# Softmax attention on Trainium2: queries kept in an order by half and class modulo 4, and keys copied into that order on the chip

## The chip, the cores and the metric

The kernel runs on one NeuronCore of a Trainium2 chip. The metric is the device time of one execution in microseconds (us), here the median of three runs. The engines are TensorE (PE: matmuls; PEld: its weight loads), VectorE (DVE), ScalarE (ACT), GpSimd (POOL) and SyncE (SP, which issues most DMAs). Each engine works through its own instructions in program order.

## The reference, cut to what matters

One decoder layer: SwiGLU feed-forward, a mixing block, a second feed-forward, a gated per-layer embedding. The change touches the softmax attention over the prompt of 1024 tokens, with 8 heads of 64, which is half of the mixing block.

```python
DILATED_BRANCHES = ((128, 1), (512, 4), (2048, 16))
# a query at t reads t, t-d, t-2d, ..., t-window, in every branch; the branches are merged
# with weights proportional to their softmax denominators
for window, dil in DILATED_BRANCHES:
    o, l = dilated_branch_prompt(qa, ka, va, window, dil)
    outs.append(o)
    lses.append(l)
...
att = combine_branches(outs, lses)
```

So a query needs its near keys (distance up to 128, every one) and far keys at distances that are multiples of 4 (and of 16), that is, keys of its own class modulo 4. Merging by denominators lets the kernel add log-counts as a mask and use one softmax.

## The kernel before, in words

The program runs feed-forward 1 (to about 780 us), the projections and gated linear attention (to about 1127 us), the softmax attention of the prompt (about 1127 to 1300 us, eight heads one after the other), the output projection, feed-forward 2 and the embedding. Inside the mixing block PE, ACT, DVE and POOL follow an order written out by hand: generators ("streams") are merged by declared costs (`Merge`), and small pieces of work are put off by a number of steps with `L.add(steps, ...)` and run at the end of a step by `L.tick()`. SP is not in that hand-written order; a scheduler places its DMAs.

*Storing queries and keys.* Each projected chunk of 352 tokens arrives in PSUM. `store_qk` scales it into `t`, rotates it where needed, and ACT writes a rounded part `hi` (L935); one step later `spill_qk` subtracts on DVE to get `lo` (L942). After the third chunk of a group of 128 rows, `hi` and `lo` go to DRAM (`d_q`, `d_ql`, or `d_k`) by POOL DMAs (L947 to L951). There are four such groups each of keys and queries; the last group is of queries.

*Loading a head.* `load_a` brings `KA` (128 rows: the rounded part of the keys and their remainder) and `QA` (the rounded queries twice); `load_b` brings `KB` (rounded keys again; 8 more rows hold ones) and `QB` (remainder of the queries; 8 more rows hold the negative row maxima, written by POOL in `rows`, L1446). All of these are in the order of the tokens.

*Row maxima.* `max_step` makes 9 score tiles `sm` per head (L1420, queries as weights, keys moving); DVE reduces them; PE turns the result (`pm`, L1438), ACT copies it, POOL writes it into `QB`. This runs ahead of the main work by `LEAD` = 7 tiles beyond a whole head.

*Main work.* A head has 7 tiles (`TILES`), one per step. A tile is a PSUM bank `st` of keys by queries, filled by pairs of matmuls: `KA` by `QA` (L1472) and `KB` by `QB` (L1473), keys as weights and queries moving. Tiles 0, 1 and 4 are class tiles: parts `("c", half, r, w)` take the 128 keys of class r in one half of the sequence, and 256 or 128 queries of the class, both through `tokens_of`, which steps over 4 columns. Tiles 2, 3, 5 and 6 are near tiles: a block of 128 neighbouring keys and up to 256 neighbouring queries. One step later `weigh` adds the mask on DVE (L1483, L1485) and ACT takes the exponent (L1486). Two steps after the tile `total` multiplies with the values (L1499) into one of two PSUM banks `nd`, by 512 queries each; class parts write there with a step of 4 columns. `finish1` and `finish2` divide by the denominator: four ACT instructions (L1514 to L1521), two POOL products, one DVE and one ACT instruction, one POOL subtraction.

Beside it a stream `attend_sample` works on the cache of the 8 sample sequences; it streams `kc` and `vc` tiles of 448 KB by SP and multiplies them (L1608, L1656). The main work fills the rest of PE's order:

```python
        while done < min(len(maxes), NM + LEAD + (n + 1) * NM // len(TILES)):
            max_step(*maxes[done])
            done += 1
            t += 0.2
        L.tick()
```

## Time and profile before

| | |
|---|---|
| median of 3 runs | 2269.69 us (2266.19 to 2274.14) |
| the profiled execution's own time | 2270.06 us |
| its span, first to last instruction | 2268.3 us |
| mean granted TensorE clock | 0.982 |
| PE / PEld / DVE / ACT / POOL busy | 96% / 80% / 66% / 36% / 30% |
| DMA | 426 MB, mean 188 GB/s |

The busy shares are averages over stages with different limits. A PE that is busy all the time is not PE at its peak, since the ends of matmuls are modelled; the distance from one start to the next tells what an instruction costs. The profile shows the execution that was traced; its own time lies 0.4 us above the median.

### The profile page before, as it was taken

To read this page: it belongs to the slowest core of one execution; us is meant where nothing else is said; L and a number is where in the kernel's file an instruction comes from. 1 tells how busy PE (TensorE), PEld (TensorE's weight loads), DVE (VectorE), ACT (ScalarE), POOL (GpSimd) and SP (SyncE) were. 2 spreads that over 40 slices of the span, in tenths; PEclk is the share of its full clock that TensorE was granted. 3 is DMA by queue.
4 is the path that set the end of the run, shared out by engine and by line. 5 is a ranking of instruction groups with operands and counts; after the bars stand their busy time and mean duration, and the time that the engine had idled before them with its cause. 6 is when DMAs were issued, how large, how long until landed. Compare 5 with 4: busy or idle time off the path is not lost. (4 is left out here: it accounts for less than half of the span.)

```text
span 2268.3 us, 39818 instructions
## 1 busy us (share of the span) xinstructions
PE 2180.0 (96%) x16242; PEld 1812.5 (80%) x16242; DVE 1489.0 (66%) x2446; ACT 811.9 (36%) x1397; POOL 671.8 (30%) x490
## 2 busy tenths in 40 slices
PE   7999999999999999999999998999999999999896
PEld 5788888877777899889778896778888887777796
DVE  7855655568888835764367525865565658888947
ACT  4433333333112634433155503433333333111734
POOL 0456655550000001101044200265565551000225
PEclk9999999999999999989999998999999999999898
DMA  3376676659672211235978640277667639773212
GB/s 116 118 264 236 240 247 236 219 202 355 260 260 97 89 43 51 74 133 163 302 216 243 216 157 19 69 243 252 234 238 246 235 138 391 266 268 127 70 75 105
DMA packets 137832, 426.04 MB, mean 188 GB/s; under 512 B 17168, under 2 KB 38032, under 8 KB 126896
## 3 DMA queue, kind: packets, MB, share of 16 engines
q1 hardware_dynamic: 127616, 338.79, 42.6%
q0 software_dynamic: 4864, 80.09, 10.4%
q10 hardware_dynamic: 5168, 4.61, 0.6%
q8 instruction: 128, 2.10, 0.4%
q14 instruction: 56, 0.46, 0.1%
HBM read 313.73 MB, written 176.75 MB: 216 GB/s over the span
## 5 line engine op out<-in xcount | busy, mean ns | idle before, releaser
L174 PE MATMUL acc_a_f<-xxh_f,wh_f_a 128*128 128x512 f32 x704 | 225.0, 400 | 16.7 <-ACT xxh_f L239 11.3
L174 PEld LDWEIGHTS acc_a_f<-xxh_f,wh_f_a 128*128 128x128 f32 x704 | 133.5, 190 | 51.6 <-ACT xxh_f L239 13.0
L278 POOL TENSOR_TENSOR S_f<-raw_gu_f,S_f 128x512 f32<-128x512 f32 x40 | 59.4, 1485 | 324.2 <-DVE wl_f_a L293 324.2
L174 PE MATMUL acc_a_f<-xxh_f,wl_f_a 128*128 128x512 f32 x352 | 139.8, 397 | 0.0
L293 DVE TENSOR_TENSOR wl_f_a<-raw_gu_f,wh_f_a 128x1024 fp32r<-128x1024 f32 x44 | 56.0, 1275 | 117.1 <-ACT wh_f_a L292 117.1
L174 PE MATMUL acc_c_f<-xxl_f,wh_f_a 128*128 128x512 f32 x384 | 120.5, 395 | 0.0
L273 POOL TENSOR_TENSOR S_f<-raw_gu_f 128x512 f32<-128x512 f32 x40 | 54.4, 1359 | 222.6 <-DMA raw_gu_f<-w_gu 222.4
L351 ACT ACTIVATE g_f<-acc_a_f 128x512 f32<-128x512 f32 x44 | 26.3, 598 | 243.2 <-PE acc_a_f L174 241.8
L850 PE MATMUL acc_m<-wh_m,xh_mx 128*128 128x256 f32 x384 | 112.8, 294 | 0.0
L850 PE MATMUL acc_m<-wl_m,xh_mx 128*128 128x256 f32 x384 | 109.6, 285 | 0.0
L850 PE MATMUL acc_m<-wh_m,xl_mx 128*128 128x256 f32 x384 | 109.1, 284 | 0.0
L174 PE MATMUL acc_b_f<-xd_f,wh_f_s 128*128 128x512 f32 x320 | 102.5, 402 | 4.0 <-DVE c_f L335 4.0
L174 PE MATMUL acc_b_f<-xd_f,wh_f_a 128*128 128x512 f32 x320 | 104.2, 407 | 0.0
L174 PE MATMUL acc_b_f<-xc_f,wh_f_s 128*128 128x512 f32 x320 | 99.4, 392 | 2.1 <-DVE U_f L335 2.1
L174 PE MATMUL acc_c_f<-xxl_f,wh_f_s 128*128 128x512 f32 x320 | 100.2, 394 | 0.0
L546 ACT ACTIVATE wo_f_wl<-wr_f 128x1024 fp32r<-128x1024 f32 x36 | 38.1, 1059 | 155.9 <-DVE wr_f L335 62.5
L546 ACT ACTIVATE wo_f_wh<-wr_f 128x1024 fp32r<-128x1024 f32 x34 | 36.0, 1059 | 144.6 <-DVE wr_f L335 56.7
L174 PEld LDWEIGHTS acc_c_f<-xxl_f,wh_f_a 128*128 128x128 f32 x384 | 71.9, 188 | 17.0
L661 DVE SCALAR_TENSOR_TENSOR ho_f<-acc_d_f,ho_f 128x512 f32<-128x512 f32 x88 | 60.0, 689 | 33.8 <-PE acc_d_f L174 29.4
L354 ACT ACTIVATE g_f<-g_f 128x512 f32<-128x512 f32 x44 | 27.8, 633 | 148.9 <-DVE g_f L335 148.9
L293 DVE TENSOR_TENSOR wl_f_s<-S_f,wh_f_s 128x1024 fp32r<-128x1024 f32 x40 | 76.6, 1914 | 5.5 <-ACT wh_f_s L292 5.3
L174 PEld LDWEIGHTS acc_a_f<-xxh_f,wl_f_a 128*128 128x128 f32 x352 | 66.8, 190 | 15.9
(500 smaller groups left out, 6392.0 us busy)
## 6 DMA issues: line engine op xcount, KB each, us to landing
raw_gu_f<-w_gu SPq DMA_DIRECT2D x42, 1024.0 KB, 5.4
xo_f_xh<-d_hid SPq DMA_DIRECT2D x36, 1024.0 KB, 6.5
xo_f_xl<-d_hid SPq DMA_DIRECT2D x34, 1024.0 KB, 6.5
o_kw<-k_win POOLq DMA_DIRECT2D x8, 4088.0 KB, 15.8
o_vw<-v_win POOLq DMA_DIRECT2D x8, 4088.0 KB, 15.7
d_hid<-c_f SPq DMA_DIRECT2D x88, 256.0 KB, 4.0
d_hid<-hi_f_t SPq DMA_DIRECT2D x88, 256.0 KB, 2.3
wr_f<-w_d SPq DMA_DIRECT2D x40, 512.0 KB, 5.9
```

The source lines that it names most:

```text
L174: k.nc.tensor.matmul(ps, w, x, start=first and n + i == 0, stop=last and n == len(kts) - 1 and i == 2, skip_group_check=True)
L273: pool(q.S[:, 0], q.A[:, 2], q.A[:, 3], op=ALU.add)
L278: pool(q.S[:, 1], q.A[:, 1], q.S[:, 1], op=ALU.subtract)
L293: dve(wl[:, b], src, wh[:, b].bitcast(F32), op=ALU.subtract)
L351: e2 = lambda u: act(work_tile(u, "g1"), unit(u).banks["a"], AF.Silu)
L354: e3b = lambda u: act(unit(u).g2, unit(u).g2, AF.Silu)
L546: act(w[:, 0], A[p][PRODUCTS[i][2]], AF.Copy)
L661: nc.vector.scalar_tensor_tensor(o, b, 0.5, o, op0=ALU.mult, op1=ALU.add)
L850: nc.tensor.matmul(ps[:, :256], x[:, kt, at * P:at * P + P], wt[:, kt], start=kt == 0 and m == 0, stop=kt == KT - 1 and m == 2)
```

## The change

- Queries are written to DRAM by half of the sequence and class (`by_class`: half, class r, position c) in `hi` and `lo`: the copy and the subtraction read `t` with a step of 4 columns (`turned`). A chunk that crosses the middle takes two instructions. A further ACT instruction rounds `t` in place, and the queries go a third time, in token order, to a new DRAM tensor `d_qn`, by SP.
- `load_a` brings `KA` and `NQ` (queries in token order, two buffers, for the row maxima alone); `load_b` brings `QB` and `QA` (by class, two buffers). `KB` is no longer loaded: `copy_hi` copies it from `KA` on ACT into one buffer.
- `by_class_copies` copies the keys on ACT into class order, `CA` and `CB`, half by half: 128 and 64 rows by 512 columns, read with a step of 4. They lie in columns of `xh` and `xl` (`xh_mx`, `xl_mx` in the profile), for the last head in `KA[2]` and `NQ[0]`.
- Class tiles read neighbouring columns of `CA`, `CB`, `QA` and `QB`. Near tiles read queries in four runs of 64 (or 32) neighbours (`near`), their masks are turned to that order, and their totals write `nd` with a step of 4 columns. Tile 3 is in three parts rather than two.
- The maxima are written in class order by two POOL instructions rather than one. `LEAD` is 5 rather than 7. Loads and copies stand at other steps.

```diff
+def by_class(x):
+    return x.rearrange("p (h r c) -> p h r c", h=2, r=4)
+def turned(x):
+    return x.rearrange("p (c r) -> p r c", r=4)
+def prompt_parts(which, x, t, c):
+    t0, t1 = c * CH, min(SEQ, (c + 1) * CH)
+    if not which:
+        yield x[:, t0:t1], t[:, t0:t1]
+        return
+    for half in range(2):
+        u0, u1 = max(t0, half * 512), min(t1, half * 512 + 512)
+        if u0 < u1:
+            c0 = (u0 - half * 512) // 4
+            yield by_class(x)[:, half, :, c0:c0 + (u1 - u0) // 4], turned(t[:, u0:u1])
...
-    nc.scalar.activation(hi[:, ct], t[:, ct], AF.Copy)
+    for x, y in prompt_parts(which, hi, t, c):
+        nc.scalar.activation(x, y, AF.Copy)
...
-    nc.vector.tensor_tensor(lo[:, ct], t[:, ct], hi[:, ct].bitcast(F32), op=ALU.subtract)
+    for (x, y), (z, _) in zip(prompt_parts(which, lo, t, c), prompt_parts(which, hi, t, c)):
+        nc.vector.tensor_tensor(x, y, z.bitcast(F32), op=ALU.subtract)
+    if which:
+        p = slice(c * CH, min(SEQ, (c + 1) * CH))
+        nc.scalar.activation(t[:, p].bitcast(F32R), t[:, p], AF.Copy)
...
+        nc.sync.dma_start(k.d_qn[rows], t[:, :SEQ])
         nc.gpsimd.dma_start(k.d_q[rows], hi)
         nc.gpsimd.dma_start(k.d_ql[rows], lo)
...
-LEAD = 7
+LEAD = 5
...
+def near(x, t0, n):
+    c0 = t0 % 512 // 4
+    return by_class(x)[:, t0 // 512, :, c0:c0 + n // 4]
...
-    ([(2, 256, 256), (3, 384, 256)], 0),
+    ([(2, 256, 256), (3, 384, 128), (3, 512, 128)], 0, None),
...
     def load_a(h):
-        H.KA, H.QA, H.KB, H.QB = k.KA[h % 3], k.QA[h % 3], k.KB[h % 2], k.QB[h % 2]
+        H.KA, H.NQ = k.KA[h % 3], k.NQ[h % 2]
...
-            queue.dma_start(H.QA[r].bitcast(F32), dram[1][h])
+            queue.dma_start(H.NQ[r].bitcast(F32), dram[3][h])
     def load_b(h):
-        nc.sync.dma_start(heads[h].KB[:64].bitcast(F32), dram[0][h][:64])
-        nc.sync.dma_start(heads[h].QB[:64].bitcast(F32), dram[2][h])
+        H = heads[h]
+        H.QA, H.QB = k.QA[h % 2], k.QB[h % 2]
+        nc.sync.dma_start(H.QB[:64].bitcast(F32), dram[2][h])
+        for r in (slice(0, 64), slice(64, 128)):
+            nc.sync.dma_start(H.QA[r].bitcast(F32), dram[1][h])
+    def by_class_copies(h, half):
...
+        src = turned(H.KA[:, 512 * half:512 * half + 512].bitcast(F32))
+        for x, r in ((H.CA, slice(0, P)), (H.CB, slice(0, 64))):
+            nc.scalar.activation(by_class(x[r])[:, half], src[r], AF.Copy)
+    def copy_hi(h, half):
+        cs = slice(512 * half, 512 * half + 512)
+        nc.scalar.activation(k.KB[:64, cs], heads[h].KA[:64, cs].bitcast(F32), AF.Copy)
...
-                keys, queries = tokens_of(H.KA, half, r), tokens_of(H.QA, half, r, w)
-                keys2, queries2 = tokens_of(H.KB[:72], half, r), tokens_of(H.QB[:72], half, r, w)
+                keys, keys2 = (by_class(x)[:, half, r] for x in (H.CA, H.CB[:72]))
+                queries, queries2 = (by_class(x)[:, half:, r] for x in (H.QA, H.QB[:72]))
...
-                    out = H.nd[bk][:, c0:c0 + w] if step == 1 else tokens_of(H.nd[bk], 0, c0)
+                    out = turned(H.nd[bk][:, to]) if isinstance(to, slice) else turned(H.nd[bk])[:, to]
...
     load_a(2)
+    for half in range(2):
+        by_class_copies(0, half)
+        copy_hi(0, half)
...
-            if h and i == 3 and h + 1 < NH:
+            if h and i == 0 and h + 1 < NH:
                 load_b(h + 1)
+            if h + 1 < NH:
+                if i in (2, 5):
+                    L.add(1, lambda h=h, half=i // 5: by_class_copies(h + 1, half))
+                elif i == 4:
+                    L.add(1, lambda h=h: copy_hi(h + 1, 0))
+            if i == 0 and h:
+                L.add(1, lambda h=h: copy_hi(h, 1))
```

Three places show how the instructions stand. First PE, in the sixth head: near tile 2 (with the last of its row maxima and the totals behind it) and the turned maxima `pm`, before the change.

```order
L1472 MATMUL st_12101<-QA_10915,KA_10914 128x256
L1473 MATMUL st_12101<-QB_10174,KB_10172 128x256
L1472 MATMUL st_12101<-QA_10915,KA_10914 128x256
L1473 MATMUL st_12101<-QB_10174,KB_10172 128x256
L1420 MATMUL sm_12106<-KA_10168,QA_10170 128x128
L1420 MATMUL sm_12106<-KA_10168,QA_10170 128x384
L1499 MATMUL nd_12109<-pt_12060,gl 128x128 x2
L1438 MATMUL pm_12121<-ident,mx_11823 8x128
```

The same head after the change: near tile 3, the first totals of the second bank, and then tile 4's last pair with the totals and `pm` behind it.

```order
L1521 MATMUL st_12204<-QA_10195,KA_10932 128x256
L1522 MATMUL st_12204<-QB_10199,KB 128x256
L1521 MATMUL st_12204<-QA_10195,KA_10932 128x128
L1522 MATMUL st_12204<-QB_10199,KB 128x128
L1521 MATMUL st_12204<-QA_10195,KA_10932 128x128
L1522 MATMUL st_12204<-QB_10199,KB 128x128
...
L1521 MATMUL st_12242<-QA_10195,xh_mx 128x128
L1522 MATMUL st_12242<-QB_10199,xl_mx 128x128
L1469 MATMUL sm_12251<-KA_10193,NQ_10197 128x256 x2
L1546 MATMUL nd_12176<-pt_12188,gl 128x4x64 x2
L1487 MATMUL pm_12259<-ident,mx_11878 8x128
```

Tile 3 has six matmuls instead of four, near totals write 4 runs of 64 (`128x4x64`), and `pm` has moved from behind tile 2 to behind tile 4.

Second ACT, from tile 5 of the sixth head to tile 1 of the seventh, before the change (`pt` is a tile's exponent, `fr`, `fd` and `fn` are `finish1`, `xh_mx<-fn` is `finish2`).

```order
L1486 ACTIVATE pt_12218<-pt_12218 128x512
L1514 ACTIVATE fr_12245<-nd_12109 64x512
L1515 ACTIVATE fr_12245<-fr_12245 64x512
L1516 ACTIVATE fd_12247<-nd_12109 64x512
L1521 ACTIVATE fn_12246<-nd_12109 64x512
L1486 ACTIVATE pt_12254<-pt_12254 128x384
L1486 ACTIVATE pt_12279<-pt_12279 128x512
L1529 ACTIVATE xh_mx<-fn_12246 64x512
L1486 ACTIVATE pt_12305<-pt_12305 128x512
L1514 ACTIVATE fr_12323<-nd_12154 64x512
```

The same place after the change.

```order
L1534 ACTIVATE pt_12289<-pt_12289 128x512
L1456 ACTIVATE xh_mx<-KA_10192 128x512
L1456 ACTIVATE xl_mx<-KA_10192 64x512
L1561 ACTIVATE fr_12320<-nd_12176 64x512
L1562 ACTIVATE fr_12320<-fr_12320 64x512
L1563 ACTIVATE fd_12322<-nd_12176 64x512
L1568 ACTIVATE fn_12321<-nd_12176 64x512
L1534 ACTIVATE pt_12329<-pt_12329 128x384
L1534 ACTIVATE pt_12357<-pt_12357 128x512
L1460 ACTIVATE KB<-KA_10192 64x512
L1576 ACTIVATE xh_mx<-fn_12321 64x512
L1534 ACTIVATE pt_12384<-pt_12384 128x512
```

Two class copies stand ahead of `finish1` of the first bank, and one `KB` copy ahead of `finish2`.

Third SP, the loads of one head boundary among the `vc` loads of the samples, before the change.

```order
L1652 DMA vc_11901<-c_v 128x896
L1405 DMA KA_10167<-d_k 128x1024
L1407 DMA QA_10169<-d_q 64x1024 x2
L1410 DMA KB_10172<-d_k 64x1024
L1411 DMA QB_10174<-d_ql 64x1024
L1652 DMA vc_11943<-c_v 128x896
```

The same after the change.

```order
L1438 DMA NQ_10196<-d_qn 64x1024 x2
L1709 DMA vc_11895<-c_v 128x896
L1709 DMA vc_11921<-c_v 128x896
L1709 DMA vc_11956<-c_v 128x896
L1436 DMA KA_10192<-d_k 128x1024
L1443 DMA QB_10199<-d_ql 64x1024
L1445 DMA QA_10195<-d_q 64x1024 x2
L1709 DMA vc_11994<-c_v 128x896
```

The queries for the maxima stand three `vc` loads ahead of the keys, and the queries of the main tiles stand behind the keys in place of `KB`.

## Rows read from the trace of the kernel before

**Rows 1.** Busy time by stretch: start and end in us, length, busy us (and instructions) of PE, PEld, DVE, ACT and POOL, granted clock, DMA share, GB/s. The last row is from another call of the same view.
```profile
860.00:960.00 100.00, 96.69 (x1501) 90.49 (x1500) 68.53 (x198) 40.51 (x110) 11.68 (x11) 0.98 0.18 61
...
1127.00:1207.00 80.00, 76.12 (x581) 61.70 (x584) 56.94 (x156) 44.36 (x82) 30.23 (x22) 1.00 0.78 226
1207.00:1288.00 81.00, 81.00 (x756) 67.66 (x746) 49.38 (x105) 45.92 (x82) 36.33 (x27) 1.00 0.77 232
...
1300.00:1320.00 20.00, 19.12 (x120) 18.78 (x119) 5.45 (x11) 0.74 (x3) 0.00 (x0) 1.00 0.99 367
```

**Rows 2.** Timeline of PE in the sixth and seventh head: start us, us, instruction, operands, shape, how many were merged into the row. In order: totals of class tiles 0 and 1, class tile 4, totals of near tile 2, near tiles 5 and 6, class tile 0 of the next head. A row's cost is read as the distance to the next start.
```profile
1235.60 1.50 PE L1499 MATMUL nd<-pt,gl 128*128 128x128 f32 x12
1236.94 0.61 PE L1637 MATMUL spt<-ident,s 128*128 128x128 f32 x4
1237.31 0.46 PE L1472 MATMUL st<-QA,KA 128*128 128x128 f32 x1
1237.59 0.42 PE L1473 MATMUL st<-QB,KB 72*128 72x128 f32 x1
...
1239.22 0.43 PE L1420 MATMUL sm<-KA,QA 128*128 128x512 f32 x1
1239.49 1.03 PE L1499 MATMUL nd<-pt,gl 128*128 128x256 f32 x4
1240.45 0.64 PE L1656 MATMUL spv<-vc,pT 128*32 128x128 f32 x14
1241.02 0.39 PE L1472 MATMUL st<-QA,KA 128*128 128x256 f32 x1
1241.24 0.28 PE L1473 MATMUL st<-QB,KB 72*128 72x256 f32 x1
1241.36 0.28 PE L1472 MATMUL st<-QA,KA 128*128 128x256 f32 x1
1241.48 0.28 PE L1473 MATMUL st<-QB,KB 72*128 72x256 f32 x1
1241.60 0.40 PE L1420 MATMUL sm<-KA,QA 128*128 128x512 f32 x1
...
1243.71 0.23 PE L1472 MATMUL st<-QA,KA 128*128 128x128 f32 x1
1243.78 0.27 PE L1473 MATMUL st<-QB,KB 72*128 72x128 f32 x1
1243.89 0.68 PE L1420 MATMUL sm<-KA,QA 128*128 128x512 f32 x2
...
1245.95 0.60 PE L1472 MATMUL st<-QA,KA 128*128 128x256 f32 x1
1246.37 0.42 PE L1473 MATMUL st<-QB,KB 72*128 72x256 f32 x1
1246.61 0.42 PE L1472 MATMUL st<-QA,KA 128*128 128x256 f32 x1
...
1247.08 0.42 PE L1420 MATMUL sm<-KA,QA 128*128 128x512 f32 x1
```

**Rows 3.** Who waited for whom between 1127 and 1300 us: us in total, times, longest.
```profile
ACT pt L1486 <- DVE pt L1483: 23.7, 17, 3.6
PE sm L1420 <- DMA QA<-d_q: 3.4, 2, 2.0
```

**Rows 4.** ACT and POOL groups by form: busy us, mean ns of one.
```profile
L1486 ACT ACTIVATE pt<-pt 128x512 f32<-128x512 f32 x48 | 30.2, 629 | 41.7 <-DVE pt L1483 23.7 <-DVE pt L1485 17.3
L962 ACT ACTIVATE new<-kst 32x128 f32<-32x128 f32 x4 | 1.5, 387 | 12.7 <-PE kst L961 12.7
L1642 ACT ACTIVATE pT<-spt 32x128 f32<-32x128 f32 x2 | 0.5, 250 | 0.0
L1446 POOL TENSOR_TENSOR QB<-new 8x1024 fp32r<-8x1024 f32 x8 | 15.1, 1891 | 15.8 <-ACT new L1445 15.6
```

**Rows 5.** The queries' way from the last chunk to the first row maximum: timelines of ACT, DVE, POOL, SP and PE, one or two rows each.
```profile
1064.10 0.47 ACT L935 ACTIVATE vb<-gl 128x320 fp32r<-128x320 f32 x1 [3.31 <-DVE gl L926]
...
1064.60 0.49 DVE L942 TENSOR_TENSOR vb<-gl,vb 128x320 fp32r<-128x320 f32 x1 [0.60 <-ACT vb L935]
...
1065.38 0.53 POOL L948 DMA_DIRECT2D d_ql<-vb  x1
...
1070.83 1.24 SPq L2091 DMA_DIRECT2D qs<-d_s  x2
...
1082.15 0.66 PE L1420 MATMUL sm<-KA,QA 128*128 128x128 f32 x2 [1.79 <-DMA QA<-d_q]
```

**Rows 6.** Timeline of ACT at the start of the sixth head, the exponents of tiles 0 and 1 and then `finish1` of the bank that the next totals will overwrite; in brackets the idle time ahead of an instruction.
```profile
1228.92 0.63 ACT L1486 ACTIVATE pt<-pt 128x512 f32<-128x512 f32 x1 [1.95 <-DVE pt L1483]
...
1231.84 0.63 ACT L1486 ACTIVATE pt<-pt 128x512 f32<-128x512 f32 x1 [0.96 <-DVE pt L1483]
1232.49 0.59 ACT L1514 ACTIVATE fr<-nd 64x512 f32<-64x512 f32 x1
...
1234.24 0.59 ACT L1521 ACTIVATE fn<-nd 64x512 f32<-64x512 f32 x1
```

**Rows 7.** DMA issues by tile between 1127 and 1285 us: count, KB each, median us from issue to landing; the row above them is the queue's packets, MB and share.
```profile
q1 hardware_dynamic: 14168, 34.77, 75.0%
...
QA<-d_q SPq DMA_DIRECT2D x10, 256.0 KB, 6.2
```

More of the change, by code (lines that the diff above doesn't have):

```diff
@@ L1365, in load_values @@
                             src[512 * half:512 * half + 512].rearrange("(p r) c -> p r c", r=4))
-def tokens_of(x, half, r, n=P):
-    return x[:, 512 * half:512 * half + 4 * n].rearrange("p (c r) -> p r c", r=4)[:, r]
 TILES = (
-    ([("c", 0, r, 256) for r in (0, 1)], 640),
-    ([("c", 0, r, 256) for r in (2, 3)], 640),
-    ([(0, 0, 256), (1, 128, 256)], 0),
-    ([(2, 256, 256), (3, 384, 256)], 0),
-    ([("c", 1, r, 128) for r in range(4)], 640),
-    ([(4, 512, 256), (5, 640, 256)], 0),
-    ([(6, 768, 256), (7, 896, 128)], 0),
+    ([("c", 0, r, 256) for r in (0, 1)], 512, 256),
+    ([("c", 0, r, 256) for r in (2, 3)], 512, 256),
+    ([(0, 0, 256), (1, 128, 256)], 0, 256),
+    ([(2, 256, 256), (3, 384, 128), (3, 512, 128)], 0, None),
+    ([("c", 1, r, 128) for r in range(4)], 512, 128),
+    ([(4, 512, 256), (5, 640, 256)], 0, 256),
+    ([(6, 768, 256), (7, 896, 128)], 0, None),
 )
@@ L1419, in max_step @@
             k0 = pc * 512
-            nc.tensor.matmul(ps[:, at:at + w], H.QA[:, i * P:(i + 1) * P], H.KA[:, k0:k0 + w], start=True, stop=True)
+            nc.tensor.matmul(ps[:, at:at + w], H.NQ[:, i * P:(i + 1) * P], H.KA[:, k0:k0 + w], start=True, stop=True)
             at += w
@@ L1462, in main_step @@
                 half, r, w = part[1:]
-                keys, queries = tokens_of(H.KA, half, r), tokens_of(H.QA, half, r, w)
-                keys2, queries2 = tokens_of(H.KB[:72], half, r), tokens_of(H.QB[:72], half, r, w)
-                outs = [(bk, r, 4, 8 + 4 * half + r, at + P * (bk - half)) for bk in range(half, 2)]
+                keys, keys2 = (by_class(x)[:, half, r] for x in (H.CA, H.CB[:72]))
+                queries, queries2 = (by_class(x)[:, half:, r] for x in (H.QA, H.QB[:72]))
+                outs = [(bk, r, 8 + 4 * half + r, at + P * (bk - half), P) for bk in range(half, 2)]
             else:
                 j, q0, w = part
-                kc, qc = slice(j * P, j * P + P), slice(q0, q0 + w)
-                keys, queries, keys2, queries2 = H.KA[:, kc], H.QA[:, qc], H.KB[:72, kc], H.QB[:72, qc]
-                cut = [q0, 512, q0 + w] if q0 < 512 < q0 + w else [q0, q0 + w]
-                outs = [(x // 512, x % 512, 1, j, at + x - q0, y - x) for x, y in zip(cut, cut[1:])]
+                keys, keys2 = H.KA[:, j * P:j * P + P], H.KB[:72, j * P:j * P + P]
+                queries, queries2 = (near(x, q0, w) for x in (H.QA, H.QB[:72]))
+                outs = [(q0 // 512, slice(q0 % 512, q0 % 512 + w), j, at, w)]
             nc.tensor.matmul(ps[:, at:at + w], keys, queries, start=True, stop=False, skip_group_check=True)
@@ L1492, in total @@
                     continue
-                for m, c0, step, v, at, *w in [x for x in H.sums[bk] if x[0] <= n]:
-                    w = w[0] if w else P
+                for m, to, v, at, w in [x for x in H.sums[bk] if x[0] <= n]:
                     first = H.nd[bk] is None
@@ L1548, in attend @@
     load_a(2)
+    for half in range(2):
+        by_class_copies(0, half)
+        copy_hi(0, half)
     yield 0.0, 4.0
@@ L1910, in build @@
     k.d_q = dram.tile([512, SEQ], F32R, name="d_q")
+    k.d_qn = dram.tile([512, SEQ], F32, name="d_qn")
     k.d_ql = dram.tile([512, SEQ], F32R, name="d_ql")
@@ L2078, in build @@
         k.KA, k.QA = ([k.pre.tile([P, SEQ], F32R, name=f"{n}{i}") for i in range(2)] for n in ("KA", "QA"))
-        k.KB, k.QB = ([k.pre.tile([P, SEQ], F32R, name=f"{n}{i}") for i in range(2)] for n in ("KB", "QB"))
+        k.NQ, k.QB = ([k.pre.tile([P, SEQ], F32R, name=f"{n}{i}") for i in range(2)] for n in ("NQ", "QB"))
         k.VP = [gl.rearrange("p i t -> p (i t)")[:, b:b + 16 * VW + 64] for b in (0, 16 * VW + 64)]
@@ L2093, in build @@
         k.vst, end_vst = po("vst", **right)
-        k.mT = k.vst.tile([P, 896], F32, name="mT")
+        k.mT = k.vst.tile([P, 768], F32, name="mT")
         nc.sync.dma_start(k.mT, a["c_mT"])
@@ L2116, in build @@
         k.KA.append(k.at.tile([P, SEQ], F32R, name="KA2"))
-        k.QA.append(k.at.tile([P, SEQ], F32R, name="QA2"))
+        k.KB = k.at.tile([P, SEQ], F32R, name="KB")
+        nc.gpsimd.memset(k.KB[64:72].bitcast(F32), 1.0)
         k.ready = True
@@ L2241, in layout @@
     near, far = (weight(g * (x - r), b) for g, b in ((1, BRANCHES[:1]), (4, BRANCHES[1:])))
-    put("c_mT", np.concatenate([near, near, near[:, :P], far], axis=1))
+    turn = lambda m: m.reshape(m.shape[0], -1, 4).transpose(0, 2, 1).reshape(m.shape)
+    put("c_mT", np.concatenate([turn(near), turn(near[:, :P]), turn(near[:, P:]), far], axis=1))
     put("c_mS", weight(P * 7 + r - np.arange(SEQ)[None, :]))
```

28 lines of the change are left out of this document (15 added, 13 removed).

## The prediction

> **What bounds the kernel now.** First the busy time by stretch, to see which engine leaves no gap where the change acts. [...] A head thus takes 20.2 us, and ACT has 11.5 us of work in it. Since a busy PE need not be at its peak, the timeline of PE comes next, read from start to start. It shows what class tiles cost beside near tiles that have the same number of columns: class tile 0 takes 1.13 us (1245.95 to 1247.08), near tile 5 takes 0.58 us (1241.02 to 1241.60); single matmuls follow each other after 0.24 us in the one and after 0.12 us in the other [rows 2]. Class tile 4, with eight matmuls of 128 columns, takes 1.91 us (1237.31 to 1239.22), 0.23 us for each after the first pair, although they have half of the columns; two near matmuls of 128 columns take 0.07 and 0.11 us [rows 2]. The cost of a class matmul hence goes with the 128 keys it loads as weights at a step of 4 columns, not with the queries that move. Last the waits: in the whole stretch PE waits for a transfer only 3.4 us, twice, for queries that the row maxima need [rows 3]; ACT waits for work from DVE far longer (23.7 us for one line), so it has slack. What shortens PE's own instructions here should shorten the program, until ACT or the chain of `finish1` has no slack left.
>
> **Class tiles, the gain.** After the change keys and queries of class tiles are neighbours. I price them as near tiles. Tiles 0 and 1: 1.13 - 0.58 = 0.55 us each, 1.10 us per head. Tile 4: its first matmul at 0.22 us as in near tile 5, seven more at 0.09 us (between the 0.07 and the 0.11 us above), so 0.85 us, which saves 1.06 us (0.92 to 1.20). Tile 3 is now one pair of 256 and two of 128 columns, two matmuls more: 0.22 + 0.12 + 4 x 0.09 = 0.70 instead of 0.58 us, a loss of 0.12 us (0.04 to 0.20). Per head 1.10 + 1.06 - 0.12 = 2.04 us; eight heads give **16.3 us** (14.6 to 18.4). All of this lies on PE, which has no gap there.
>
> **Totals and near queries: nothing.** Near totals now write PSUM at a step of 4 columns. Class totals already do: twelve of 128 columns follow each other after (1236.94 - 1235.60) / 12 = 0.112 us, and near totals of 256 neighbouring columns after (1240.45 - 1239.49) / 4 = 0.24 us, the same per column [rows 2]. The rows thus show no price for that step, so I take zero. [...] What it would cost if the near totals doubled is worked out among the rivals. Queries read in runs of 64 neighbours: no row has such runs; the class tiles, whose queries stepped by 4, were set by their weights, so I take no price.
>
> **ACT, the new load.** Per head come four class copies (512 columns read at a step of 4) and two `KB` copies. A plain one of 512 columns costs 0.63 us [rows 4]. For a stepped one, the lower bound is the same 0.63 us; the nearest row of ACT at a step is the copy of 32x128 that writes at a step, 0.39 us against 0.25 us for a plain one of that size [rows 4], so 0.14 us more for 128 columns and 0.56 us for 512: 1.19 us. I take 1.1 us, near that row, since its step is real. Per head: 4 x 1.1 + 2 x 0.63 = 5.7 us, so ACT has 11.5 + 5.7 = 17.2 us of work, and PE 20.2 - 2.0 = 18.2 us. ACT still fits, but with a share of 95%. What is late first is the chain of `finish1`: in the sixth head the copy `fn` that frees the second `nd` bank ends at 1234.83 us [rows 6], and PE's first total into that bank comes after two of the twelve that begin at 1235.60 (each instruction is two records), at about 1236.05 [rows 2]: 1.2 us of slack. Two class copies now stand ahead of the first bank's `finish1`, one `KB` copy ahead of the exponents, and the two class tiles between lose 1.1 us. ACT idled 1.95 and 0.96 us ahead of the exponents before it [rows 6]. 2.2 + 0.6 us of copies and 1.1 us of lost time, 3.9 us, stand against 1.2 us of slack and 2.9 us of idle time, 4.1 us: just within. Since not all idle time can be used, I take **+2 us** over the eight heads (0 to 5, the upper end with 0.7 us per head).
>
> **POOL.** The maxima go into `QB` in two instructions of 512 elements instead of one of 1024 at 1.89 us [rows 4]. With `LEAD` 5 they come two steps later, behind tile 4. From there to the next head's second matmul are tiles 5 and 6, some 6 us (1240.45 to 1246.37 [rows 2]). PE to ACT to POOL needs 0.27 us for the copy, about 1.5 us in ACT's queue, and 1.9 to 3.8 us on POOL (the upper end: each half as dear as the whole). It fits: 0 (up to 3).
>
> **Loads.** `NQ` adds 512 KB per head and `KB` drops 256 KB: 8 x 256 KB = 2 MB on 34.8 MB of that queue [rows 7], and the queue has room (226 GB/s in the stretch, 367 GB/s a little later [rows 1]). `NQ` has a free buffer early, so it stands three loads ahead of the keys, and the maxima of the next but one head begin a step later (`LEAD`). Both waits of 3.4 us in total should go; queries landed 6.2 us after their issue [rows 7], a step is 20.2 / 7 = 2.9 us. I take **-3 us** (-3.4 to 0).
>
> **Storing the queries.** Twelve query chunks get one more ACT instruction (about 0.5 us) and stepped reads in two; in this part ACT is at 40.5 of 100 us [rows 1], so most is hidden: **+1 us** (0 to 3). The last chunk's is not. Its copy (1064.10), subtraction (1064.60), store (1065.38), the loads that begin when the store has landed (1070.83), and the first row maximum (1082.15, which PE awaited for 1.79 us) form one chain [rows 5]. Whatever it grows by PE waits. Two stepped instructions of 320 columns at the price above cost 320/512 x 0.56 = 0.35 us more each, the rounding is off that chain or 0.5 us, and a third 512 KB store beside two takes up to 512 KB / 367 GB/s = 1.4 us: **+2 us** (0 to 4).
>
> **Sum.** -16.3 + 2 - 3 + 1 + 2 = -14.3 us. Against the profiled execution's own 2270.06 us (span 2268.3) that is 2255.8 us; the median of the runs is 0.4 us lower, so 2255.4. The ends: -18.4 - 3.4 gives 2248; -14.6 + 5 + 3 + 3 + 4 = +0.4 if every price is at its worst together, which I do not expect; two or three of them leave 2263.
>
> **Rivals.**
> A, ACT becomes the bound. If a stepped copy costs more than 1.84 us, ACT has 11.5 + 1.26 + 4 x 1.84 = 20.1 us per head and nothing is left of the gain. At 1.5 us (18.8 us, and about 1 us per head that the in-order queue waits) 0.4 us per head is left: some 2266 us with the start's cost. At 2.2 us it is 21.6 us per head, 1.4 us more than now: 2270 + 8 x 1.4 + 2 = 2283 us, slower. For it: the step made weight loads two to three times as dear [rows 2]. Against it: the one ACT row at a step. [...]
> B, the PSUM writes. If near totals cost double at a step, 15 records of 256 columns (twelve, and six of 128) at 0.24 us are 3.6 us per head, 29 us in all: 2284 us, slower. It decides from half of that. Against it stands the equal price per column above.
> C, the change doesn't shorten the class tiles, since something other than the stepped weights sets their pace (the 4-byte step of the queries is gone as well, so hardly). Then 2270 + 2 - 3 + 3 = 2272 us at most, within or just outside of what can be told from now.
> D, the start eats more: the chain of the last queries grows by 8 us instead of 2 because the three stores queue behind each other: 2262 us.
>
> **How the numbers follow.** Forecast with all its prices, 2247 to 2262: 0.70. A in its mild form, 2263 to 2268: 0.11; A in its hard form, about 2283: 0.05. B: 0.03. C: 0.03. D, 2260 to 2265: 0.08. A measurement of this kernel tells about 0.3%, 6.8 us, from no change. Faster takes the forecast and most of D: 0.77; same takes mild A, the rest of D and most of C: 0.15; slower takes hard A and B: 0.08. The range that holds 8 in 10 is 2247 to 2266 us.
>
> **What would show it.** Class tiles of 0.6 us and tile 4 of 0.7 to 1.0 us from start to start; near totals still at 0.22 to 0.24 us; no wait of row maxima for queries after 1127 us; the class copies on ACT at 0.63 to 1.2 us; the first row maximum awaited longer than before. I am wrong if those copies take 1.8 us or more, if PE shows gaps of over 0.5 us per head ahead of the totals or of tile 0, or if a matmul at a step in PSUM is slower.

## The result, and the profile after

The changed kernel takes 2296.16 us (median of 4 runs, 2286.7 to 2298.1) against 2268.6 us of the kernel before on the same chip: ratio 1.011, 95% interval 1.0076 to 1.0143. It is **slower by 27.6 us**, 1.1%; the forecast was 2255.4 us, within 2247 to 2266, so both the sign and the range were wrong.

The profiled execution took 2286.7 us, the quickest of the four, so what follows explains some 17 us of the 27.6. Of the rest only this is known: the others had a mean granted clock of 0.970 to 0.971 instead of 0.977.

Outside of attention nothing changed. From the transposition that ends the samples' attention to the last instruction it is 965.6 us before and 964.2 us after; the first row maximum starts at 1082.15 and at 1081.93 us (the wait ahead of it has grown, but the part of the program before that was quicker in this execution). So I compare the stage between these two points. Busy time by stretch, first the kernel before, then the changed one (start and end in us, length, busy us and instructions of PE, PEld, DVE, ACT and POOL, granted clock, DMA share, GB/s):

```profile
1082.15:1302.66 220.51, 215.85 (x1834) 179.75 (x1834) 132.42 (x342) 103.26 (x187) 71.28 (x55) 0.99 0.80 243
```

```profile
1081.93:1320.66 238.73, 215.87 (x1849) 174.22 (x1850) 127.54 (x342) 142.23 (x235) 78.99 (x65) 0.93 0.75 230
...
1127.00:1207.00 80.00, 69.46 (x487) 53.10 (x488) 45.64 (x127) 54.88 (x92) 26.56 (x21) 0.85 0.72 209
1207.00:1288.00 81.00, 71.79 (x687) 57.90 (x686) 51.62 (x129) 65.95 (x108) 42.05 (x33) 0.98 0.74 225
```

From such a row I take three numbers, for this and for all kernels below. **Idle**: length less PE's busy time, 4.7 us before and 22.9 us after. **Clock**: length times (1 - granted clock), what the granted clock lacks of 1.00 over the stage, 2.2 and 16.7 us (the clock has two digits, so this is good to 1.2 us; where PE also waits in such a stretch it counts some time twice). **Rest**: what remains, the work of PE as at a granted clock of 1.00, 213.6 and 199.2 us. By this reading the work has become 14.5 us shorter. Read in steps of 0.25 us the granted clock of both stages is 1.00 or 0.50 (half clock) but for the edges between the two; where half clock during a wait isn't counted twice, the gain is 12.4 us (214.2 and 201.8 us; half clock is 15.6 us, 1.6 of them in waits). So the work gives about three quarters or more of the gain that was forecast; 18.2 us of idle time and some 14 us of half clock take it back twice over. In the two stretches from 1127 to 1288 us PE, busy for 76.12 and 81.0 us before [rows 1], has 10.5 and 9.2 us without work.

The tiles did become what they should. Timeline of PE in the changed kernel: class tile 4, a row maximum, and the first class tile of the next head:

```profile
1252.50 0.33 PE L1521 MATMUL st<-QA,xh_mx 128*128 128x128 f32 x1
...
1253.44 0.45 PE L1469 MATMUL sm<-KA,NQ 128*128 128x256 f32 x2
1253.73 1.03 PE L1546 MATMUL nd<-pt,gl 128*128 128x256 f32 x4
...
1260.04 0.38 PE L1521 MATMUL st<-QA,xh_mx 128*128 128x256 f32 x1
...
1260.62 0.40 PE L1469 MATMUL sm<-KA,NQ 128*128 128x512 f32 x1
```

Tile 4 takes 0.94 us from start to start (1252.50 to 1253.44) instead of 1.91, tile 0 0.58 us instead of 1.13 [rows 2]; four near totals of 256 columns, which now write at a step of 4, take 1.03 us as before [rows 2]. The copies cost what was forecast, and POOL's two row instructions too. ACT and POOL groups between 1127 and 1290 us (busy us, mean ns of one):

```profile
L1456 ACT ACTIVATE xl_mx<-KA 64x512 fp32r<-64x512 f32 x14 | 15.6, 1111 | 0.0
L1456 ACT ACTIVATE xh_mx<-KA 128x512 fp32r<-128x512 f32 x13 | 14.6, 1125 | 0.0
L1460 ACT ACTIVATE KB<-KA 64x512 fp32r<-64x512 f32 x16 | 9.8, 615 | 0.0
L1497 POOL TENSOR_TENSOR QB<-new 8x512 fp32r<-8x512 f32 x14 | 18.0, 1303 | 22.4 <-ACT new L1494 22.3
```

Who waited for whom in the stage after (us in total, times, longest); before, PE's entry for the row maxima was 3.4 us, for `QA` [rows 3]. The 5.1 us for `NQ` end where the stage begins, and are not in its idle time:

```profile
DVE xl_mx L1366 <- ACT xh_mx L1365: 29.9, 11, 5.3
...
PE spv L1713 <- DMA vc<-c_v: 6.3, 3, 4.8
...
PE sm L1469 <- DMA NQ<-d_qn: 5.1, 1, 5.1
...
PE st L1521 <- DVE pt L1531: 4.0, 2, 3.2
...
PE sm L1469 <- ACT pT L1699: 3.2, 1, 3.2
...
PEld st L1522 <- POOL QB L1497: 2.8, 1, 2.8
```

One of these gaps, followed through. Timeline of ACT:

```profile
1180.64 0.59 ACT L1561 ACTIVATE fr<-nd 64x512 f32<-64x512 f32 x1
...
1182.41 0.59 ACT L1568 ACTIVATE fn<-nd 64x512 f32<-64x512 f32 x1
1182.90 0.62 ACT L1534 ACTIVATE pt<-pt 128x512 f32<-128x512 f32 x1
1183.42 1.11 ACT L1456 ACTIVATE xh_mx<-KA 128x512 fp32r<-128x512 f32 x1
1184.43 1.10 ACT L1456 ACTIVATE xl_mx<-KA 64x512 fp32r<-64x512 f32 x1
1185.43 0.47 ACT L1698 ACTIVATE pT<-spt 128x384 f32<-128x384 f32 x1
1185.81 0.25 ACT L1699 ACTIVATE pT<-spt 32x128 f32<-32x128 f32 x1
```

and of PE:

```profile
1182.44 0.45 PE L1469 MATMUL sm<-KA,NQ 128*128 128x512 f32 x1
1186.11 0.90 PE L1469 MATMUL sm<-KA,NQ 128*128 128x128 f32 x2 [3.22 <-ACT pT L1699]
```

Busy time of the stretch that follows, and of one other like it (the granted clock is the third number from the end):

```profile
1184.90:1195.10 10.20, 8.99 (x41) 7.02 (x45) 5.43 (x17) 4.27 (x9) 1.40 (x2) 0.50 0.44 122
1133.80:1140.50 6.70, 6.70 (x33) 5.60 (x33) 3.80 (x14) 3.69 (x6) 0.00 (x0) 0.50 0.54 172
```

The next row maximum needs a PSUM bank that holds four transposed blocks of the samples (`spt`), and ACT is to copy them out. In ACT's queue that copy stands behind `finish1`, one exponent and two class copies, an unbroken run of 4.8 us in which ACT has no idle time; the two copies are 2.2 us of it. PE stands still for 3.2 us, and from 1184.90 to 1195.10 us its granted clock is 0.50, although it has work for 9 of these 10.2 us. Such stretches at 0.50 lie in the changed kernel's attention behind the gaps at 1128.7 (3.6 us from start to start, DVE behind the six first copies), 1156.6 (0.50 from 1157.7 to 1164.4 us), 1182.4 and 1237.9 us (5.2 us, `vc`; 0.50 from 1243.0 to 1246.25 us), and there is one where the stage begins (to 1085.75 us), as in the kernel before (1082.5 to 1085.75 us).

### The profile page after: what moved, and what is told of

Its sections match the earlier page's. It is cut to its first block, busy times and chain, and to the rows that moved or that the text cites. A ratio compares the mean times of both kernels' runs of the same rounds, so it can differ in the third digit from the quotient of the medians.

```text
span 2284.9 us, 39944 instructions
## 1 busy us (share of the span) xinstructions
PE 2176.0 (95%) x16258; PEld 1804.4 (79%) x16258; DVE 1487.5 (65%) x2450; ACT 860.3 (38%) x1461; POOL 677.3 (30%) x499
## 5 line engine op out<-in xcount | busy, mean ns | idle before, releaser
L174 PE MATMUL acc_a_f<-xxh_f,wh_f_a 128*128 128x512 f32 x704 | 225.0, 400 | 16.7 <-ACT xxh_f L239 11.3
L174 PEld LDWEIGHTS acc_a_f<-xxh_f,wl_f_a 128*128 128x128 f32 x352 | 66.8, 190 | 15.9
## 6 DMA issues: line engine op xcount, KB each, us to landing
o_kw<-k_win POOLq DMA_DIRECT2D x8, 4088.0 KB, 15.6
```

What stands on the lines that cost most here:

```text
L174: k.nc.tensor.matmul(ps, w, x, start=first and n + i == 0, stop=last and n == len(kts) - 1 and i == 2, skip_group_check=True)
```

## Experiments

Times are medians of 4 to 12 executions; "beside" is the kernel before in the same job (13 to 23 executions; 4 beside the changed kernel); stage, idle, clock and rest are of the one profiled execution, as worked out above. No difference reaches 2%; one whose interval leaves out 1 is clear of the noise.

| kernel | us | against before beside it | ratio, 95% interval | stage | idle | clock | rest |
|---|---|---|---|---|---|---|---|
| before | 2268.6 | | | 220.5 | 4.7 | 2.2 | 213.6 |
| changed | 2296.2 | +27.6 | 1.0076 to 1.0143 | 238.7 | 22.9 | 16.7 | 199.2 |
| a_nocopy | 2277.4 | +8.8 | 1.0026 to 1.0057 | 232.5 | 18.5 | 16.3 | 197.8 |
| a_plain | 2282.3 | +13.7 | 1.0037 to 1.0072 | 234.0 | 18.6 | 16.4 | 199.0 |
| b_copies | 2282.6 | +14.0 | 1.0036 to 1.0074 | 231.9 | 10.2 | 7.0 | 214.8 |
| a_lead7 | 2286.4 | +17.8 | 1.0039 to 1.0090 | 232.8 | 21.9 | 11.6 | 199.2 |
| a_loads | 2290.7 | +23.2 | 1.0085 to 1.0115 | 242.4 | 21.6 | 21.8 | 198.9 |
| n_loads | 2272.6 | +5.1 | 1.0009 to 1.0031 | 219.3 | 13.9 | 4.4 | 201.0 |
| a_pool | 2283.3 | +15.9 | 1.0050 to 1.0084 | 230.2 | 16.3 | 16.1 | 197.8 |
| c1 | 2278.3 | +10.8 | 1.0031 to 1.0060 | 223.1 | 13.7 | 6.7 | 202.7 |
| b_init | 2272.3 | +4.7 | 1.0008 to 1.0034 | 225.1 | 6.6 | 4.5 | 214.0 |
| a_raw | 2288.7 | +21.1 | 1.0078 to 1.0111 | 240.1 | 21.1 | 21.6 | 197.4 |
| c2 | 2269.8 | +2.2 | 0.9999 to 1.0019 | 218.9 | 11.1 | 6.6 | 201.2 |
| b_keys | 2265.3 | -3.6 | 0.9974 to 1.0001 | 216.5 | 7.9 | 2.2 | 206.5 |
| b_keys_act | 2272.3 | +3.4 | 1.0007 to 1.0026 | 221.3 | 10.4 | 4.4 | 206.5 |
| b_half | 2263.5 | -5.4 | 0.9965 to 0.9990 | 215.7 | 5.1 | 4.3 | 206.3 |

The rest takes three values, 214 to 215 us with the tiles of before, 197 to 203 us with all class tiles short, 206 us with the keys alone in class order. Read in steps of 0.25 us as above, these are 214.0 to 215.1, 199.7 to 202.0 and 206.3 to 207.2 us. What an edit does to the time is in the two columns ahead of it.

### a_nocopy: the changed kernel without copies

```diff
-        src = turned(H.KA[:, 512 * half:512 * half + 512].bitcast(F32))
-        for x, r in ((H.CA, slice(0, P)), (H.CB, slice(0, 64))):
-            nc.scalar.activation(by_class(x[r])[:, half], src[r], AF.Copy)
+            H.CA, H.CB, H.KB = H.KA, k.KB, k.KB
...
-        nc.scalar.activation(k.KB[:64, cs], heads[h].KA[:64, cs].bitcast(F32), AF.Copy)
+        if h == 0:
+            nc.scalar.activation(k.KB[:64, cs], heads[h].KA[:64, cs].bitcast(F32), AF.Copy)
```

Two plain `KB` copies ahead of head 0 stay.

> The changed kernel without the copies into class order: class tiles read their 128 keys from neighbouring columns of the natural keys (wrong tokens, the same shapes and the same number of instructions), and the second stationary block is filled once, by two copies for head 0. Left out: about 5.7 us of ScalarE work per head and 4.5 us ahead of head 0. Theory 1 (ScalarE's in-order queue: the copies push back the exponentials, the rows for the maxima, the finishing steps and the evictions that stand behind them, and TensorE waits): nearly the whole loss goes; attention keeps its shorter class tiles (-16 us) and what is left of the loss is 3.4 us in the start chain, some 5 us for one late load of value cache rows and 3 us for the last row of maxima: 2255 to 2266 us, the granted clock at full level between 1127 and 1288 us. Theory 2 (loads and their order on SyncE's queue, or the shorter lead of the maxima of 5, make the waits): the time stays above 2285 us.

2277.38 us, in neither band. Neither theory holds alone: by the medians the copies make about 19 of the 27.6 us, and 9 us over before remain although 15 us of TensorE's work is gone. The traces show less of it: the profiled execution here was the longest of its ten (2284.7 us), that of the changed kernel the shortest of its four, and between these two the stage differs by 6.2 us. PE's waits for transfers in the profiled execution:

```profile
PE sm L1464 <- DMA NQ<-d_qn: 8.7, 2, 4.6
PE spv L1708 <- DMA vc<-c_v: 5.5, 2, 3.5
...
PE ss L1660 <- DMA kc<-c_k: 2.1, 2, 1.1
```

Of the 8.7 us for `NQ` 4.6 lie in the stage; with `vc` and `kc` that makes 12.2 of its 18.5 us of idle time. Those 4.6 us are new: with the copies gone, the maxima of head 2 come before their queries (`NQ`, whose load is issued from 1129.4 us on and takes up to 11.4 us to land).

### a_plain: the copies as plain neighbours

```diff
-            nc.scalar.activation(by_class(x[r])[:, half], src[r], AF.Copy)
+            nc.scalar.activation(x[r, cs], H.KA[r, cs].bitcast(F32), AF.Copy)
```

> The changed kernel with the copies into class order read and written as plain neighbours (the output is not the reference's, since class tiles then hold other tokens): by the 615 ns of the plain copy of 64 partitions each of the four class copies per head falls from 1.12 to 0.62 us, so that ScalarE has 3.7 us of copies per head instead of 5.7. Theory 1 (ScalarE's queue): the loss falls by about a third to a half, 2278 to 2290 us. Theory 2 (loads, lead): no change, 2290 to 2300 us.

2282.25 us, as theory 1 has it: 2.0 us of ScalarE's work per head (16 us in all) are worth about 14 us of time by the medians. In the profiled executions the stage is 4.7 us shorter than in the changed kernel.

### b_copies: the kernel before with the copies

```diff
...
+                if i in (2, 5):
+                    L.add(1, lambda h=h, half=i // 5: by_class_copies(h + 1, half))
+                elif i == 4:
+                    L.add(1, lambda h=h: copy_hi(h + 1, 0))
+            if i == 0 and h:
+                L.add(1, lambda h=h: copy_hi(h, 1))
```

The six copies ahead of head 0 are in it too.

> The kernel before with the changed kernel's six ScalarE copies per head added at the same places of the program, into buffers that nothing reads; all else as before. Theory 1 (ScalarE's queue): slower by 10 to 30 us, 2279 to 2298 us, with waits of TensorE on ScalarE's evictions and of VectorE on ScalarE that the kernel before does not have. Theory 2 (loads, lead): within 4 us of before, 2265 to 2273 us.

2282.61 us: 14.0 us slower, with nothing but ScalarE's extra work. Busy time of the stage:

```profile
1080.79:1312.70 231.91, 221.75 (x1833) 184.00 (x1834) 133.88 (x342) 143.38 (x235) 72.04 (x55) 0.97 0.74 231
```

Two of its waits (us in total, times, longest); the first is 12.0 us in the kernel before, the second is of a kind that it doesn't show:

```profile
DVE xl_mx L1349 <- ACT xh_mx L1348: 21.5, 11, 5.2
...
PE st L1494 <- DVE pt L1505: 3.4, 1, 3.4
```

ACT is busy for 143 of 232 us, 62% of the stage, and costs 14 us all the same. This is the plainest evidence against pricing ACT by its share.

### b_init: only the six copies ahead of head 0

```diff
     load_a(2)
+    for half in range(2):
+        by_class_copies(0, half)
+        copy_hi(0, half)
```

> The kernel before with only the six copies ahead of head 0 added (5.1 us of ScalarE in one piece, into buffers that nothing reads), nothing per head. Theory 4 (a gap of TensorE costs more than its own length, since a stretch of half clock follows it): one gap of 2 to 4 us near 1128 us, a half-clock stretch of 6.8 us right behind it, which costs about 3 us more, and none elsewhere in attention: 2273 to 2277 us. If the half clock is not set off by gaps: 2270 to 2272 us, and no half clock near 1130 us.

2272.29 us, 4.7 us more. Timeline of PE at the gap:

```profile
1129.65 0.43 PE L1442 MATMUL sm<-KA,QA 128*128 128x512 f32 x1
1133.45 0.58 PE L1494 MATMUL st<-QA,KA 128*128 128x256 f32 x1 [3.38 <-DVE pt L1505]
```

Busy time of the stretch behind it and of the stage:

```profile
1132.60:1139.30 6.70, 5.85 (x29) 4.72 (x29) 5.07 (x15) 2.35 (x5) 1.89 (x1) 0.50 0.34 124
...
1081.62:1306.69 225.07, 218.50 (x1834) 181.61 (x1834) 131.99 (x342) 108.46 (x192) 71.28 (x55) 0.98 0.76 237
```

Place, length and the half clock behind it are as expected: the granted clock is 0.50 from 1132.60 to 1139.30 us, where the kernel before has 1.00 [rows 1]. The time itself is below theory 4's band and only 0.3 us above the other one, so it is the trace that decides. The stage grew by 4.6 us: idle time by 1.9 us (the gap is 3.4 us, but there is less idle time elsewhere) and half clock by 2.3 us. So here the clock costs about as much again as the added idle time, and the program grew by 1.4 times the gap.

Half clock doesn't stand behind every gap: behind the one of 3.0 us at 1275.8 us in the changed kernel the granted clock is 1.00 (1246.5 to 1320 us), and behind the waits of up to 2.0 us in the kernel before [rows 3] it is 1.00 too (1127 to 1300 us). What sets it off is not shown.

### a_lead7, a_loads, a_raw: one cause of lateness each

```diff
-LEAD = 5
+LEAD = 7
```

> The changed kernel with the lead of the maxima at 7 steps, as in the kernel before, instead of 5. Theory 3 (the shorter lead makes the rows of maxima late): 3 to 8 us shorter than the changed kernel, and TensorE's wait of 2.6 us on the row of head 7 gone. Theory 1: the wait at head 7 may go, the rest stays: 2290 to 2298 us.

2286.38 us. PE's wait for the row of head 7 is gone, and that may be worth more than the 3 to 8 us expected, but this interval and that of the changed kernel overlap. Other waits stand in its place: 3.6 us for `NQ` inside the stage, and 5.7 us of the turned maxima `pm` for DVE.

```diff
+            if i == 4 and h + 3 < NH:
+                load_n(h + 3)
-            if h and i == 0 and h + 1 < NH:
+            if h and i == 3 and h + 1 < NH:
                 load_b(h + 1)
```

> The changed kernel with its copies, and two loads moved: the naturally ordered queries of a head are asked for as soon as the maxima that used their buffer are issued (half a head earlier), and the class-ordered queries three steps later in the head, where the kernel before had its second load, so that SyncE's queue does not stand in front of the value cache rows. Theory 2 (loads): the waits on NQ behind head 0 and on vc (5.2 us) go, and with them a half-clock stretch: 6 to 14 us shorter, 2282 to 2290 us. Theory 1 (ScalarE's queue makes most of the loss): 0 to 5 us shorter, 2291 to 2296 us.

2290.65 us: 4 us less against its own before, as theory 1 says, within the uncertainty of the two. With the copies in place the loads alone give little: PE's longest wait for `vc` falls from 4.8 to 2.5 us, that for `NQ` ahead of the first maximum is still 5.3 us.

```diff
+    if which and c == NCH - 1:
+        nc.sync.dma_start(k.d_qn[i * P:(i + 1) * P], t[:, :SEQ])
...
-        nc.scalar.activation(t[:, p].bitcast(F32R), t[:, p], AF.Copy)
```

> The changed kernel with the natural-order queries stored unrounded (they serve only the maxima, which cancel in the division) and ahead of the class-order copies: 12 roundings of 0.5 us fewer on ScalarE, and the last store leaves before the last copy and subtraction. Theory 5 (the start chain): the wait for the first maximum falls from 5.1 us to 1.5 us or less, with a shorter half-clock stretch behind it: 4 to 7 us shorter than the changed kernel, 2288 to 2292 us. If another store or the load of the keys ends that chain, the wait stays above 4 us and the time above 2293 us.

2288.67 us is in the band of theory 5, but not by its mechanism. The gap ahead of the first maximum, 5.4 us from start to start in the changed kernel, is still 4.0 us, and the stage is no shorter (240.1 us). As idle time the gap is 3.7 us here and 4.5 us in c2, which has the same edit, but 3.5 and 3.6 us in n_loads and c1 without it. So the end of the last store isn't what sets that gap; what does was not settled.

### n_loads: loads moved, and no copies

The edits of a_nocopy and a_loads together.

> The same two moved loads in the kernel without copies (class tiles on wrong tokens, copies into class order left out). If copies and loads together make the loss, directly and by the half-clock stretches that follow each gap of TensorE, this has the 16 us of shorter class tiles and hardly a loss: 2254 to 2266 us, and fewer than 10 us of half clock between 1082 us and the end of attention. If the shorter class tiles simply leave TensorE waiting for other engines, it stays within 3 us of the kernel without copies: 2274 to 2280 us.

2272.55 us, 5 us less than a_nocopy, which is neither of the two bands. Busy time of the stage:

```profile
1083.72:1303.01 219.29, 205.39 (x1850) 166.25 (x1850) 128.44 (x342) 104.10 (x188) 77.24 (x63) 0.98 0.83 250
```

PE's waits (the one for `NQ` ends where the stage begins):

```profile
PE spv L1718 <- DMA vc<-c_v: 4.7, 3, 3.7
PE sm L1468 <- DMA NQ<-d_qn: 3.5, 1, 3.5
PE ss L1670 <- DMA kc<-c_k: 2.5, 4, 0.9
...
PE st L1521 <- POOL QB L1496: 1.9, 1, 1.9
PE sm L1468 <- DVE mx L1476: 1.7, 2, 1.5
...
PE nd L1545 <- ACT fn L1567: 1.4, 2, 1.1
```

Here TensorE's work is 12.6 us shorter than before and the stage only 1.2 us: 9.2 us reappear as idle time and 2.2 us as half clock, spread over the five causes shown and smaller ones. Transfers are 7.2 us of its idle time, at a DMA share of 0.83 where before had 0.80. The faster PE met the next limits at once.

### a_pool, c1, c2: copies on GpSimd

```diff
-            nc.scalar.activation(by_class(x[r])[:, half], src[r], AF.Copy)
+            nc.gpsimd.tensor_copy(by_class(x[r])[:, half], src[r])
```

> The changed kernel with the four class copies per head on GpSimd instead of ScalarE; the two plain copies stay on ScalarE. GpSimd's time for a 512-element stepped copy is not in the traces; its other 512-element steps take 1.27 to 1.31 us, which would give 5.2 us per head beside its 10.1. Theory 1 (ScalarE's queue): 8 to 18 us shorter than the changed kernel, 2278 to 2288 us. If GpSimd takes over 2.2 us each it is busy for nearly the whole head and the rows of maxima are late: 2290 us or more.

> Both: the class copies on GpSimd and the two loads moved; all of the computation is done. Copies and loads together: 2258 to 2274 us. If only one of the causes matters, as for the better of the two single edits, 2278 us or more.

> Class copies on GpSimd, both loads moved, the natural-order queries stored unrounded and early, and the lead of the maxima 7: all of the computation is done. From the version with the first two (2278 us, whose profiled execution was 2270): the start chain gives 3 to 4 us, the row of head 7 up to 3 us, each with part of a half-clock stretch: 2262 to 2272 us. At the upper end the loss is elsewhere: waits of TensorE on VectorE and ScalarE inside the heads.

2283.31, 2278.25 and 2269.81 us. On GpSimd a class copy takes nearly the time that it takes on ScalarE; POOL's groups in c1:

```profile
L1460 POOL CAST xl_mx<-KA 64x512 fp32r<-64x512 f32 x14 | 16.7, 1191 | 0.0
L1460 POOL CAST xh_mx<-KA 128x512 fp32r<-128x512 f32 x13 | 15.2, 1166 | 0.6
```

Moving them there takes back some 12 us, the loads another 5, start and lead 8 to 9. With all four c2 is level with before: its stage is 1.6 us shorter, with 6.4 us more idle time and 4.4 us more half clock than before. c1 missed its band by 4 us and lies at the edge of the other one, in which one cause alone matters; but it is 12 us below a_loads and 5 us below a_pool (the intervals of these last two overlap).

### b_keys, b_keys_act, b_half: only the keys

The copies stand where the changed kernel has them, on GpSimd in b_keys:

```diff
-                keys, queries = tokens_of(H.KA, half, r), tokens_of(H.QA, half, r, w)
+                keys, keys2 = (by_class(x)[:, half, r] for x in (H.CA, H.CB[:72]))
+                queries, queries2 = (tokens_of(x, half, r, w) for x in (H.QA, H.QB[:72]))
```

> The kernel before with only the keys copied into class order (the four class copies per head, on GpSimd); queries stay in their natural order, so that class tiles read stationary keys from neighbouring columns and moving queries at a step of 4, and nothing is stored or loaded differently. If the step of the stationary side made the long class tiles (its weight loads take 256 ns at a step of 4 and 120 to 195 ns otherwise), tiles 0 and 1 fall from 1.13 to 0.6 us and tile 4 from 1.94 to 0.95 us here too, and the storing of queries by class was not needed: 2255 to 2265 us, or up to 2270 us if the gaps of the version with copies on GpSimd (1.97, 1.7 and 1.66 us on VectorE and ScalarE) come again. If the moving side made them, the tiles stay at 1.0 us or more and the time is at or above that of before, 2268 to 2276 us.

2265.28 us. The tiles answer the question in two ways. Timeline of PE, tile 0 and tile 4 of the seventh head:

```profile
1238.74 0.48 PE L1492 MATMUL st<-QA,xh_mx 128*128 128x256 f32 x1
1239.04 0.41 PE L1493 MATMUL st<-QB,xl_mx 72*128 72x256 f32 x1
1239.27 0.41 PE L1492 MATMUL st<-QA,xh_mx 128*128 128x256 f32 x1
...
1239.73 0.42 PE L1440 MATMUL sm<-KA,QA 128*128 128x512 f32 x1
...
1247.93 0.36 PE L1492 MATMUL st<-QA,xh_mx 128*128 128x128 f32 x1
1248.09 0.32 PE L1493 MATMUL st<-QB,xl_mx 72*128 72x128 f32 x1
1248.21 0.32 PE L1492 MATMUL st<-QA,xh_mx 128*128 128x128 f32 x1
```

Tile 4 has its whole gain: its matmuls of 128 queries follow each other after 0.12 us, with keys in place and queries at a step of 4. Tile 0 is still 0.99 us: matmuls of 256 queries at a step follow after 0.23 us, twice the 0.12 us of near tile 5 [rows 2]. So the step in the moving columns alone holds a matmul of 256 columns at 0.23 us. With weights at a step too, the 128-column matmuls of tile 4 took the same 0.23 us [rows 2], which is thus the price of the weights. A matmul of 256 neighbouring columns with weights at a step is in no run.

> The version with only the keys copied into class order, with the four copies per head on ScalarE instead of GpSimd; nothing else differs. Theory 1 (ScalarE's queue): the copies (4.5 us per head, of the 5.7 that cost the kernel before 14 us) take back the 9 us that the shorter tiles give, and more: 2268 to 2276 us, with TensorE waits on ScalarE's results and half-clock stretches inside attention. If the engine does not matter, it is within 2 us of the version on GpSimd, 2263 to 2267 us.

2272.33 us, 7.0 us more than b_keys by their differences from before, with the engine of four copies per head as the only difference between the two, and a stage that is 4.8 us longer, half of it idle time and half the clock. Rows of the stage, first on GpSimd, then on ScalarE:

```profile
1079.04:1295.52 216.48, 208.62 (x1834) 169.08 (x1834) 134.57 (x342) 103.37 (x187) 110.63 (x89) 0.99 0.79 248
```

```profile
1082.85:1304.12 221.27, 210.89 (x1834) 170.91 (x1834) 133.43 (x342) 134.61 (x218) 73.97 (x57) 0.98 0.78 240
```

Against b_keys:

```diff
-            if h + 1 < NH and i in (2, 5):
+            if h + 1 < NH and i == 5:
...
```

> The version with only the keys copied, on GpSimd, and of these only the second half (two copies per head, for tile 4); tiles 0 and 1 read their keys at a step of 4 again and are 1.13 us instead of 1.0. Two tiles of 8 heads give 2 us back; GpSimd has 2.3 us less work per head. If the copies on GpSimd cost nothing, 2265 to 2268 us; if they delayed the finishing steps behind them, 2260 to 2264 us.

2263.52 us, ratio 0.9977 (0.9965 to 0.9990): the quickest of all, and quicker than before beyond its interval. Two copies per head on GpSimd, for tile 4 alone, and tiles 0 and 1 as before; its stage has hardly more idle time than that of before. The time lies in the band by which the other two copies delayed what stood behind them, but its interval overlaps that of b_keys, so this isn't shown.

## Why the prediction was wrong

**Class tiles, -16.3 us: nearly right as work, wrong as time.** The rest gives 12 to 15 us, and from start to start the 56 tiles take 51.4 us before and 36.3 us in n_loads, 15.1 us less. The step that failed is the sentence "All of this lies on PE, which has no gap there" (between 1207 and 1288 us [rows 1]). That a PE is busy throughout says that nothing else is late at its present pace; it doesn't say how much sooner the others could be. n_loads measures that: of 12.6 us of work saved with none of the copies per head, 1.2 us of the stage.

**ACT, +2 us (0 to 5): this is the term that was mis-sized**, at 14 us (b_copies) to 19 us (changed less a_nocopy). The price of a copy was right (1.1 us forecast, 1.11 and 1.13 us measured), and the sum of ACT's work too. Wrong was to weigh it as capacity, 17.2 of 18.2 us (from 11.5 and 20.2 us per head, a quarter of what [rows 1] have from 1207 to 1288 us, the last four heads), and to follow one chain, that of `finish1`. ACT's queue holds other things that PE or DVE wait for, in order: the evictions `pT` and `xh_mx`, the rows, the six copies ahead of head 0, which stood in the diff and were not priced at all (4.7 of the 14 us, by b_init). a_plain, b_keys_act and a_pool show it three more times.

**Missing altogether: the clock.** The prediction counted each wait by its own length. In the changed kernel half clock takes some 14 us more than before, next to 18.2 us of added idle time. b_init shows one gap with one such stretch behind it.

**Loads, -3 us: the wait it named went, another came.** No maximum waits for a transfer behind 1127 us, as forecast; but PE waits for `vc` for 4.8 us once. This `vc` is issued at 1236.65 us, behind the four issues of `KA`, `QB` and `QA` that begin at 1234.46 us; the one of `KA` had held up SyncE's queue for 6.6 us until PE was done with the buffer (2.6 us at the longest before). **Storing the queries, +1 us (0 to 3):** not to be told. The first row maximum starts between 1080.1 and 1086.7 us in the kernels that store the queries in the new way, and between 1079.0 and 1085.0 us in the others. **Start chain, +2 us (0 to 4):** the wait of 1.79 us [rows 5] became 5.1, +3.3 us, in the range; its cause was put at the store, which a_raw doesn't bear out. **POOL, 0 (up to 3):** the row of head 7 was 2.8 us late, at the upper end. **Totals, 0:** right, and rival B is out.

**The rivals.** A in its hard form was nearest in its cause (2283 us, ACT), with the wrong condition: 1.84 us per copy was not needed, 1.12 were enough. The test that was to show the prediction wrong, gaps of more than 0.5 us per head, was close to the right one: idle time grew by 18.2 / 8 = 2.3 us per head. It looked ahead of totals and of tile 0, though. Ahead of totals there are 2.7 us in all, and 2.6 us for the row inside tile 0 of head 7; the larger gaps stood ahead of row maxima, of tile 2 of head 0 and of `vc`.

**The first reading of rows 2**, that the price "goes with the 128 keys it loads as weights", was half of the truth (b_keys). It did no harm to the sum, since the change removes both steps, but it hid a cheaper change: tile 4 alone needs only the keys.

**Still open:** why the unprofiled runs of the changed kernel are 9 to 11 us above the profiled one (in c1 it is up to 15 us; a lower granted clock is all that is known of them), and with it how much of the 14 to 19 us for the copies lies where the trace shows it; and what ends the start chain.
